# One tile per streamed weight block, and all leading products ahead of the remainders

## The chip, the cores and the metric

One core of a Trainium2 chip runs the whole program. The metric is the device time of one execution in microseconds (us).

## What is computed

One layer of a hybrid backbone block over 256 latent tokens and 256 context tokens of 2048 channels, everything in float32:

```python
u = rmsnorm(x, norm_g) * (1 + scale) + shift        # scale, shift, gt = silu(c) @ w_ada + b_ada
a, g, z_c, xr, z_r, gc, gr = split(u @ w_in)
v = a * sigmoid(g)                                  # 31-tap depthwise convolution along grid rows
v = silu(layernorm(conv(v)))                        # LayerNorm over the 2048 channels
y_conv = (v * silu(z_c)) @ w_conv_out
xc = conv4(xr); r, i = sigmoid(xc @ w_r), sigmoid(xc @ w_i)     # per direction, 16 blocks of 128
h = scan(a = exp(-8 r softplus(-lam)), b = sqrt(1 - a * a) * i * xc)
y_rnn = ((h_forward + h_backward) * silu(z_r)) @ w_rnn_out
y = sigmoid(gc) * y_conv + sigmoid(gr) * y_rnn
out = rmsnorm(x + gt * (y @ w_o), final_g)          # latents only
```

## The kernel before

The weights are streamed once, in 152 **blocks** of 128 x 2048 float32 (1 MB each): 136 that give 128 output channels (accumulator `acc`, products on line 234) and 16 for `w_o` (accumulators `o`, line 912). Every float32 product is made of three: an operand is split into a **leading part** (`whi`, a copy to a shorter format on ScalarE, ACT, line 180) and a **remainder** (`wlo` = weight - leading part, a subtraction on VectorE, DVE, line 185). TensorE (PE) adds `whi * xh + whi * xl + wlo * xh`, with `xh`, `xl` the two parts of the activations. A 128-channel block of 256 tokens has 16 channel tiles, so 32 products with `whi` and 16 with `wlo`.

Before, a block is two **half blocks** of 128 x 1024, each with its own load (SyncE's queue, SP, line 175), copy and subtraction, in pools of 4 buffers (`wraw`, `whl`). `slot()` runs one block: it issues the loads of block s + 3, then for each half 16 leading products and 8 remainders on PE, the copy of the same half of block s + 2 with the subtraction of the half before it (`stage_split`), the deferred steps (`run_deferred`) and some side work of ACT and DVE (`run_side`, with a budget in us). Each engine takes its instructions in the order of the program, so what stands ahead of a subtraction on DVE delays it.

Before the blocks comes the start: adaLN's sums from `w_ada` (64 loads of 512 KB into 8 buffers `adaraw`, products on line 209) alternate with the products of the first eight xr blocks, whose weights are 16 tiles of 512 KB (`wearly`). The blocks then go: xr and z_r with the recurrence (gates on line 472: float32 products of their own), the convolution's blocks a and g, `w_rnn_out` with its gate (blocks 104 to 119), `w_conv_out` (120 to 135), `w_o` (136 to 151).

Three pieces of side work matter below. **The LayerNorm** of the convolution ends inside block 108: its variance is summed over channels by PE (`tot`, line 717), copied to `var` (line 718), and `rsqrt` (ACT's Sqrt on line 196, then DVE's reciprocal and a Newton step on lines 197 to 201) gives `rstd`, with which DVE multiplies `cv` (line 767). **gt** of adaLN, 64 steps of 512 columns on DVE (line 820), reads tiles `gtraw` of 1024 columns, two of them loaded ahead, so four steps. **The evacuation of w_o** after each 512-column chunk is three DVE operations and one of ACT per token tile (lines 896 to 899).

Of the kernel before, what the change touches and what calls it, by code (L numbers as in the profile page):

```python
# [81 lines left out]
def block_kernel(ctx, tc, xcat, xtok, fgrow, par, wada, wgt, bgt, wearly, wall, wgate, out):  # L82
# [283 lines left out]
    def stage_load(s):  # L366
        if s < NS:
            raws[s] = [load(wall[s, h]) for h in range(2)]
# [655 lines left out]
```

## Time and profile before

| | |
|---|---|
| runs | 1146.59, 1145.22, 1146.40 us; median 1146.40 |
| profiled execution: span, first to last instruction | 1142.0 us |
| median of the runs less that span | 4.4 us |
| PE busy | 1121.5 us, 98% of the span |
| DVE busy | 924.9 us, 81% |
| ACT busy | 615.1 us, 54% |
| moved by DMA | 233.70 MB, 205 GB/s in the mean |

The profiled execution is recorded by its span alone; its own time is not listed apart from the runs, so the 4.4 us that lie around the span are those of the median run. How to read it: an engine's busy time says how much work it has; which engine sets the end is told by the chain of waits and by PE's list of waits. Starts are microseconds from the first instruction. L with a number is a line of the kernel before.

### The profile page before, as it was taken

The numbers are of one execution on the slowest core, as the hardware profiler recorded it, in microseconds if no ns is written. First come the engines' busy times: TensorE is split into PE (matmuls) and PEld (weight loads), VectorE is DVE, ScalarE is ACT, GpSimd is POOL, SyncE is SP. The second block draws the span as 40 slices with busy tenths as digits, with TensorE's granted clock in tenths as the row PEclk, the third lists the DMA queues.
The fourth block names the chain that finished last, engine by engine and source line by source line (L and its number), as shares of the span: only waits on it lengthen the run. The fifth ranks groups of instructions, "written<-read, shape, count | busy, mean of one in ns | idle before, by whom it ended". The sixth has DMA issues, their size and how long they took to land.

```text
span 1142.0 us, 20720 instructions
## 1 busy us (share of the span) xinstructions
PE 1121.5 (98%) x8316; PEld 1010.7 (88%) x8316; DVE 924.9 (81%) x1528; ACT 615.1 (54%) x838; POOL 0.2 (0%) x4
## 2 busy tenths in 40 slices
PE   6999999999999999999999999999999999999996
PEld 3777778777798989999999999999999999999885
DVE  5555588789879888899998989999985977888885
ACT  3222279777888877644454444443335854444443
POOL 0000000000000000000000000000000000000000
PEclk9999999999999999999999999999999999999999
DMA  9998444233346555465555555555554569888772
GB/s 376 400 409 324 189 134 134 102 125 125 106 141 196 160 167 164 143 209 184 185 185 171 183 183 185 175 183 178 181 188 150 169 205 324 316 310 285 268 279 93
DMA packets 67635, 233.70 MB, mean 205 GB/s; under 512 B 7505, under 2 KB 11729, under 8 KB 67153
## 3 DMA queue, kind: packets, MB, share of 16 engines
q1 hardware_dynamic: 67538, 232.37, 59.5%
q8 instruction: 65, 1.06, 0.4%
q14 instruction: 32, 0.26, 0.1%
HBM read 230.25 MB, written 2.10 MB: 203 GB/s over the span
## 4 chain that ended last, share of the span: by engine, by line
PE 98%; DVE 1%; DMA 0%; ACT 0%; issue 0%; ACTq 0%; SPq 0%; DVEq 0%
PE acc L234 72%; PE o L912 8%; PE xr L234 6%; PE gate L472 5%; PE ada L209 2%; PE part L234 2%; PE ms L228 1%; DMA hbuf<-in_xcat_dram 0%; PE tp L216 0%; PE mps L228 0%; PE gps L833 0%; PE vps L228 0%; DVE sq L259 0%; DVE wlo L171 0%; PE tot L279 0%
## 5 line engine op out<-in xcount | busy, mean ns | idle before, releaser
L234 PE MATMUL acc<-xh,whi 128*128 128x256 f32 (+1 forms) x2176 | 566.8, 296 | 0.0
L234 PE MATMUL acc<-xl,whi 128*128 128x256 f32 (+1 forms) x2176 | 552.3, 289 | 0.0
L180 ACT ACTIVATE whi<-raw 128x1024 fp32r<-128x1024 f32 x304 | 321.1, 1058 | 351.0 <-PE acc L234 277.3
L234 PEld LDWEIGHTS acc<-xh,whi 128*128 128x128 f32 x2176 | 416.7, 192 | 17.8 <-issue 9.3
L234 PEld LDWEIGHTS acc<-xl,whi 128*128 128x128 f32 x2176 | 416.9, 192 | 12.5 <-issue 7.7
L185 DVE TENSOR_TENSOR wlo<-raw,whi 128x1024 fp32r<-128x1024 f32 x304 | 371.0, 1223 | 70.0 <-ACT whi L180 66.3
L234 PE MATMUL acc<-xh,wlo 128*128 128x256 f32 (+1 forms) x2176 | 319.0, 289 | 0.0
L234 PEld LDWEIGHTS acc<-xh,wlo 128*128 128x128 f32 x2176 | 288.2, 192 | 5.0
L660 DVE SCALAR_TENSOR_TENSOR cv<-hbuf,pt,cv 128x196 f32<-128x196 f32 (+14 forms) x480 | 185.9, 451 | 13.0 <-ACT cv L651 12.6
L461 DVE SCALAR_TENSOR_TENSOR xc<-xr,pt,xc 128x510 f32<-128x510 f32 (+2 forms) x96 | 71.0, 742 | 0.2
L472 PE MATMUL gate<-xc,gw 128*128 128x512 f32 x128 | 60.0, 592 | 0.0
L820 DVE SCALAR_TENSOR_TENSOR zc<-gtraw,csil,zc 128x512 f32<-128x512 f32 x64 | 47.9, 748 | 5.4 <-DMA gtraw<-in_wgt_dram 4.7
L234 PE MATMUL xr<-xh,whi 128*128 128x512 f32 x96 | 40.4, 421 | 0.4 <-ACT xh L170 0.4
L912 PE MATMUL o<-whi,xh 128*128 128x512 f32 x128 | 40.6, 399 | 0.0
L498 DVE TENSOR_TENSOR_SCAN tr<-a,ti 128x512 f32<-128x512 f32 x32 | 39.1, 1223 | 0.7
L333 ACT ACTIVATE row<-ada 128x128 f32<-128x128 f32 (+1 forms) x22 | 7.2, 326 | 60.2 <-PE ada L209 60.2
L912 PE MATMUL o<-whi,xl 128*128 128x512 f32 x128 | 39.5, 389 | 0.0
L912 PE MATMUL o<-wlo,xh 128*128 128x512 f32 x128 | 39.4, 389 | 0.0
L234 PE MATMUL xr<-xl,whi 128*128 128x512 f32 x96 | 37.7, 392 | 0.2 <-DVE xl L171 0.2
L472 PEld LDWEIGHTS gate<-xc,gw 128*128 128x128 f32 x128 | 22.8, 189 | 17.0 <-issue 13.9
L234 PE MATMUL xr<-xh,wlo 128*128 128x512 f32 x96 | 37.4, 390 | 0.0
L209 PE MATMUL ada<-adaraw,csil 128*32 128x128 f32 (+1 forms) x704 | 32.5, 324 | 1.1 <-DVE sh L218 0.9
(169 smaller groups left out, 838.1 us busy)
## 6 DMA issues: line engine op xcount, KB each, us to landing
raw<-in_wall_dram SPq DMA_DIRECT2D x304, 512.0 KB, 3.5
adaraw<-in_wada_dram SPq DMA_DIRECT2D x64, 512.0 KB, 8.5
gtraw<-in_wgt_dram SPq DMA_DIRECT2D x32, 512.0 KB, 3.9
raw<-in_wearly_dram SPq DMA_DIRECT2D x16, 512.0 KB, 9.9
gw<-in_wgate_dram SPq DMA_DIRECT2D x32, 128.0 KB, 3.2
hbuf<-in_xcat_dram SPq DMA_DIRECT2D x2, 1024.0 KB, 7.1
cv<-in_xtok_dram SPq DMA_DIRECT2D x4, 512.0 KB, 5.8
out_dram<-cv SPq DMA_DIRECT2D x6, 256.0 KB, 2.6
```

What stands on the lines that cost most here:

```text
L180: A.activation(out=hi, in_=raw, func=AF.Copy)
L185: V.tensor_tensor(out=lo, in0=raw, in1=hi.bitcast(F32), op=SUB)
L209: PE.matmul(out=acc[g:g + 32, :w], lhsT=csil[:, k, :], rhs=raw[:, w * q:w * q + w], start=(k < 4), stop=(k >= KT - 4), tile_position=(0, g))
L228: PE.matmul(out=acc[32 * q:32 * q + 32, :], lhsT=ones[:, :32], rhs=x, start=(i < 4), stop=(i >= KT - 4), tile_position=(0, 32 * q))
L234: PE.matmul(out=acc, lhsT=w, rhs=x, start=(first and i == 0), stop=(last and i == n - 1))
L333: A.activation(out=row, in_=acc, func=AF.Copy)
L461: V.scalar_tensor_tensor(out=o, in0=i, scalar=w, in1=o, op0=MUL, op1=ADD)
L472: PE.matmul(out=acc, lhsT=u["gw"][:, c:c + 128], rhs=u["xc"], start=True, stop=True)
L498: V.tensor_tensor_scan(out=r(u["tr"]), data0=r(u["a"]), data1=r(u["ti"]), initial=0.0, op0=MUL, op1=ADD)
L660: V.scalar_tensor_tensor(out=o, in0=i, scalar=hdw[:, m * CW + j:m * CW + j + 1], in1=o, op0=MUL, op1=ADD)
L820: V.scalar_tensor_tensor(out=gt_chunk(c), in0=gt_raw[0][:, 512 * (k % 2):512 * (k % 2) + 512], scalar=csil[:, k, 0:1], in1=gt_chunk(c), op ...
L912: PE.matmul(out=acc, lhsT=y[:, k, 1, P * i:P * i + P], rhs=w[:, 512 * kk:512 * kk + 512], start=(k == 0 and w is hi and y is xh), stop=(k ...
```

## The change

A block is one tile of 128 x 2048, with one load of 1 MB, one copy and one subtraction (152 of each instead of 304), in 3 buffers of raw weights and 2 of each part (before: 4 halves of each). `staged()` replaces the two halves: the load of block s + 3; all 32 leading products; deferred steps and side work; the subtraction of block s + 1 and the copy of block s + 2; all 16 remainders; deferred steps and side work again. `w_o`'s blocks follow the same pattern, with both token tiles' leading products (8 each) ahead of both tiles' remainders (4 each). The early xr weights come in one load, one copy and one subtraction per group of one or two channel tiles.

The raw tiles take 8 KB more of each partition, and other buffers are cut: `adaraw` 8 to 6, the squares `sq` of the LayerNorm 8 to 4, `gtraw` from two tiles of 1024 columns to two of 512 (64 loads of 256 KB, two steps ahead), and `var` is dropped (ACT's Sqrt and DVE's Newton step read the sum `tot` in PSUM). PE's products are the same in number.

```diff
+RB = 3
...
-    wraw_p = ctx.enter_context(tc.tile_pool(name="wraw", bufs=4))
-    whl_p = ctx.enter_context(tc.tile_pool(name="whl", bufs=4))
+    wraw_p = ctx.enter_context(tc.tile_pool(name="wraw", bufs=RB))
+    whl_p = ctx.enter_context(tc.tile_pool(name="whl", bufs=2))
...
-    def load(src, n=1024):
-        raw = wraw_p.tile([P, 1024], F32, tag="raw", name="raw")
+    def load(src, n=2048):
+        raw = wraw_p.tile([P, 2048], F32, tag="raw", name="raw")
         SP.dma_start(out=raw[:, :n], in_=src)
         return raw
 
-    def wsplit_hi(raw):
-        hi = whl_p.tile([P, 1024], F32R, tag="whi", name="whi")
-        A.activation(out=hi, in_=raw, func=AF.Copy)
+    def wsplit_hi(raw, n=2048):
+        hi = whl_p.tile([P, 2048], F32R, tag="whi", name="whi")
+        A.activation(out=hi[:, :n], in_=raw[:, :n], func=AF.Copy)
         return hi
 
-    def wsplit_lo(raw, hi):
-        lo = whl_p.tile([P, 1024], F32R, tag="wlo", name="wlo")
-        V.tensor_tensor(out=lo, in0=raw, in1=hi.bitcast(F32), op=SUB)
+    def wsplit_lo(raw, hi, n=2048):
+        lo = whl_p.tile([P, 2048], F32R, tag="wlo", name="wlo")
+        V.tensor_tensor(out=lo[:, :n], in0=raw[:, :n], in1=hi[:, :n].bitcast(F32), op=SUB)
         return lo
 
-    def wsplit(raw, n=1024):
-        hi = whl_p.tile([P, 1024], F32R, tag="whi", name="whi")
-        lo = whl_p.tile([P, 1024], F32R, tag="wlo", name="wlo")
-        split(hi[:, :n], lo[:, :n], raw[:, :n])
-        return hi, lo
...
-        ada_p = st.enter_context(tc.tile_pool(name="ada", bufs=8))
+        ada_p = st.enter_context(tc.tile_pool(name="ada", bufs=6))
...
-                    wr = [load(wearly[k], P * NEARLY) for k in ks]
+                    wn = P * NEARLY * n
+                    wr = wraw_p.tile([P, 2048], F32, tag="raw", name="raw")
+                    SP.dma_start(out=wr[:, :wn].rearrange("p (k c) -> p k c", k=n), in_=wearly[:, k0:k0 + n, :])
...
-                    ws = [wsplit(w, P * NEARLY) for w in wr]
+                    hi = wsplit_hi(wr, wn)
+                    ws = (hi, wsplit_lo(wr, hi, wn))
...
-            raws[s] = [load(wall[s, h]) for h in range(2)]
-
-    late = []
-
-    def stage_split(s, h):
-        """the weights' leading parts; the remainders of the half block before"""
-        for k, raw, hi in late:
-            parts[k] = (hi, wsplit_lo(raw, hi))
-        late.clear()
+            raws[s] = load(wall[s])
+
+    def stage_hi(s):
         if s < NS:
-            raw = raws[s][h]
-            late.append(((s, h), raw, wsplit_hi(raw)))
-
-    def block_mms(s, acc, movh, movl, half):
-        hi, lo = parts.pop((s, half))
-        tr3 = []
-        for kk in range(8):
-            k = 8 * half + kk
-            w = hi[:, 128 * kk:128 * kk + 128]
-            tr3 += [(w, movh(k)), (w, movl(k))]
-        for kk in range(8):
-            tr3 += [(lo[:, 128 * kk:128 * kk + 128], movh(8 * half + kk))]
-        mm3(acc, half == 0, half == 1, tr3)
+            his[s] = wsplit_hi(raws[s])
+
+    def stage_lo(s):
+        if s < NS:
+            los[s] = wsplit_lo(raws.pop(s), his[s])
+
+    def block_mms(acc, ws, movs, first, last):
+        for k in range(KT):
+            for mov in movs:
+                PE.matmul(out=acc, lhsT=ws[:, P * k:P * k + P], rhs=mov(k), start=(first and k == 0 and mov is movs[0]),
+                          stop=(last and k == KT - 1))
+
+    def staged(s, leading, remainders, work):
+
+        stage_load(s + RB)
+        leading(his[s])
+        run_deferred()
+        work()
+        stage_lo(s + 1)
+        stage_hi(s + 2)
+        remainders(los[s])
+        del his[s], los[s]
+        run_deferred()
+        work()
...
-        """matrix products of block s, the weights of the blocks after it, side work"""
         acc = psum(f"acc{s}")
         view = acc[:, :N] if N == T else acc.rearrange("p (s t) -> p s t", s=2)
-        stage_load(s + 3)
-        for h in range(2):
-            block_mms(s, view, *mov, h)
-            stage_split(s + 2, h)
-            run_deferred()
-            run_side(budget / 2)
+        staged(s, lambda w: block_mms(view, w, mov, True, False), lambda w: block_mms(view, w, mov[:1], False, True),
+               lambda: run_side(budget / 2))
...
+    def chunk_mms(acc, w, seg, ys, kq, i, first, last):
+
+        for kk in range(4):
+            k = 4 * kq + kk
+            for y in ys:
+                PE.matmul(out=acc, lhsT=y[:, k, seg, P * i:P * i + P], rhs=w[:, 512 * kk:512 * kk + 512],
+                          start=(first and k == 0 and y is xh), stop=(last and k == KT - 1))
+
+    def chunk_slot(s, seg, accs, kq, work):
+
+        def leading(w):
+            for i in range(2):
+                chunk_mms(accs[i], w, seg, (xh, xl), kq, i, True, False)
+
+        def remainders(w):
+            for i in range(2):
+                chunk_mms(accs[i], w, seg, (xh,), kq, i, False, True)
+        staged(s, leading, remainders, work)
...
-            stage_split(1, 0)
+            stage_hi(1)
...
-    stage_split(1, 1)
...
-    def ln_total(dst):
+    def ln_total():
         tot = psum("tot")[:, :T]
         PE.matmul(out=tot, lhsT=sel4, rhs=ln["rstd"], start=True, stop=True)
-        V.tensor_copy(dst, tot)
+        return tot
 
     def ln_mean2():
-        ln_total(ln["mean"])
+        V.tensor_copy(ln["mean"], ln_total())
...
-        sq = tp2.tile([P, T], F32, tag="sq", name="sq", bufs=8)
+        sq = tp2.tile([P, T], F32, tag="sq", name="sq", bufs=4)
...
-        ln_total(ln["var"])
-        rsqrt(ln["rstd"], ln["mean"], ln["var"])
+        rsqrt(ln["rstd"], ln["mean"], ln_total())
...
-        raw = tp2.tile([P, 1024], F32, tag="gtraw", name="gtraw", bufs=GTB)
+        raw = tp2.tile([P, 512], F32, tag="gtraw", name="gtraw", bufs=GTB)
...
-        V.scalar_tensor_tensor(out=gt_chunk(c), in0=gt_raw[0][:, 512 * (k % 2):512 * (k % 2) + 512],
-                               scalar=csil[:, k, 0:1], in1=gt_chunk(c), op0=MUL, op1=ADD)
-        if n % 2:
-            gt_raw.popleft()
-            if n // 2 + GTB < 32:
-                gt_load(n // 2 + GTB)
+        V.scalar_tensor_tensor(out=gt_chunk(c), in0=gt_raw.popleft(), scalar=csil[:, k, 0:1],
+                               in1=gt_chunk(c), op0=MUL, op1=ADD)
+        if n + GTB < 4 * KT:
+            gt_load(n + GTB)
...
         for kq in range(2 if c == 3 else 4):
-            stage_load(s + 3)
-            for h in range(2):
-                for i in range(2):
-                    o_mms(accs[i], s, kq, h, i)
-                del parts[s, h]
-                stage_split(s + 2, h)
-                gt_steps(GTO)
+            chunk_slot(s, 1, accs, kq, lambda: gt_steps(GTO))
...
-    # the last two blocks: one token tile after the other
-    stage_split(NS, 0)
+
+    stage_lo(s + 1)
     for i in range(2):
         for q in range(2):
-            for h in range(2):
-                o_mms(accs[i], s + q, 2 + q, h, i)
+            chunk_mms(accs[i], his[s + q], 1, (xh, xl), 2 + q, i, False, False)
+            chunk_mms(accs[i], los[s + q], 1, (xh,), 2 + q, i, False, True)
```

**PE, where the LayerNorm's sum is made**, inside block 108 (`acc108`; `tot` is the sum, `whi`/`wlo` the weights' parts, numbers are tiles). Before:

```order
L234 MATMUL acc108_9733<-xl_97,whi_9612 128x256
L234 MATMUL acc108_9733<-xh_96,wlo_9653 128x256 x8
L717 MATMUL tot_9766<-rstd_5034,sel4_73 128x256
L234 MATMUL acc108_9733<-xh_96,whi_9655 128x256
L234 MATMUL acc108_9733<-xl_97,whi_9655 128x256
```

and with the change:

```order
L380 MATMUL acc108_9040<-xh_96,whi_8952 128x256
L380 MATMUL acc108_9040<-xl_97,whi_8952 128x256
L734 MATMUL tot_9075<-rstd_4738,sel4_73 128x256
L380 MATMUL acc108_9040<-xh_96,wlo_9018 128x256 x16
L380 MATMUL acc109_9115<-xh_96,whi_9020 128x256
```

The sum moves from the middle of the block's products to behind its last leading product; the remainders of block 109 then read `wlo_9090`.

**DVE in the same place** (`rstd_...<-vps` is the copy that feeds the sum, `wlo` are subtractions; `wlo_9727` and `wlo_9762` are the two halves of block 109). Before:

```order
L185 TENSOR_TENSOR wlo_9727<-raw_9582,whi_9699 128x1024
L739 COPY rstd_5034<-vps_9526 128x256
L185 TENSOR_TENSOR wlo_9762<-raw_9584,whi_9729 128x1024
L718 COPY var_5036<-tot_9766 128x256
L197 RECIPROCAL rstd_5034<-rstd_5034 128x256
L198 TENSOR_TENSOR mean_5035<-rstd_5034 128x256
L199 SCALAR_TENSOR_TENSOR mean_5035<-var_5036,mean_5035 128x256
L200 TENSOR_SCALAR mean_5035<-mean_5035 128x256
L201 TENSOR_TENSOR rstd_5034<-rstd_5034,mean_5035 128x256
L767 TENSOR_TENSOR cv_5031<-cv_5031,rstd_5034 128x256 x2
L771 TENSOR_TENSOR cv_5031<-cv_5031,zc_5032 128x256
L767 TENSOR_TENSOR cv_5031<-cv_5031,rstd_5034 128x256
```

and with the change:

```order
L186 TENSOR_TENSOR wlo_9018<-raw_8819,whi_8952 128x2048
L756 COPY rstd_4738<-vps_8853 128x256
L192 RECIPROCAL rstd_4738<-rstd_4738 128x256
L193 TENSOR_TENSOR mean_4739<-rstd_4738 128x256
L194 SCALAR_TENSOR_TENSOR mean_4739<-tot_9075,mean_4739 128x256
L195 TENSOR_SCALAR mean_4739<-mean_4739 128x256
L196 TENSOR_TENSOR rstd_4738<-rstd_4738,mean_4739 128x256
L783 TENSOR_TENSOR cv_4735<-cv_4735,rstd_4738 128x256 x2
L787 TENSOR_TENSOR cv_4735<-cv_4735,zc_4736 128x256
L783 TENSOR_TENSOR cv_4735<-cv_4735,rstd_4738 128x256
L186 TENSOR_TENSOR wlo_9090<-raw_8901,whi_9020 128x2048
```

Before, both halves of block 109's remainder are made ahead of the reciprocal, and the next subtraction behind it (`wlo_9806`) is of block 110. With the change the whole remainder of block 109 (`wlo_9090`) stands behind the reciprocal, the Newton step and four operations of the normalisation; the copy of `tot` is gone.

## Rows read from the trace of the kernel before

**Rows 1.** The page: busy time and instructions of the engines; the chain, share by engine.
```profile
PE 1121.5 (98%) x8316; PEld 1010.7 (88%) x8316; DVE 924.9 (81%) x1528; ACT 615.1 (54%) x838; POOL 0.2 (0%) x4
...
PE 98%; DVE 1%; DMA 0%; ACT 0%; issue 0%; ACTq 0%; SPq 0%; DVEq 0%
```

**Rows 2.** The last row of PE's list of waits (us in total, times, longest us).
```profile
PE xr L234 <- DVE xl L171: 0.2, 1, 0.2
```

**Rows 3.** Windows: us, then PE, PEld, DVE, ACT, POOL busy (instructions), clock, DMA share, GB/s.
```profile
0.00:100.00 100.00, 88.78 (x811) 60.35 (x812) 56.04 (x117) 30.59 (x51) 0.20 (x4) 1.00 0.98 386
...
600.00:800.00 200.00, 200.00 (x1660) 197.82 (x1659) 181.66 (x344) 87.47 (x105) 0.00 (x0) 1.00 0.56 180
```

**Rows 4.** PE in order of time, blocks 108 and 109 (start us, us, engine, line, operation).
```profile
880.28 0.28 PE L234 MATMUL acc<-xh,whi 128*128 128x256 f32 x1
...
883.15 0.59 PE L717 MATMUL tot<-rstd,sel 128*128 128x256 f32 x2
883.40 0.47 PE L234 MATMUL acc<-xh,whi 128*128 128x256 f32 x1
883.70 0.28 PE L234 MATMUL acc<-xl,whi 128*128 128x256 f32 x1
...
886.45 0.28 PE L234 MATMUL acc<-xh,whi 128*128 128x256 f32 x1
```

**Rows 5.** DVE in order of time, the same stretch.
```profile
883.78 0.42 DVE L718 COPY var<-tot 128x256 f32<-128x256 f32 x1 [1.95 <-PE tot L717]
885.36 1.75 DVE L197 RECIPROCAL rstd<-rstd 128x256 f32<-128x256 f32 x1 [1.15 <-ACT rstd L196]
...
890.63 1.22 DVE L185 TENSOR_TENSOR wlo<-raw,whi 128x1024 fp32r<-128x1024 f32 x1
```

**Rows 6.** ACT in order of time, the same stretch.
```profile
883.52 1.28 ACT L196 ACT_TABLE_LOAD   x1
884.82 0.51 ACT L196 ACTIVATE rstd<-var,epst 128x256 f32<-128x256 f32 x1
```

**Rows 7.** The page: the group of gt's steps (busy us, mean ns of one | idle before, releaser).
```profile
L820 DVE SCALAR_TENSOR_TENSOR zc<-gtraw,csil,zc 128x512 f32<-128x512 f32 x64 | 47.9, 748 | 5.4 <-DMA gtraw<-in_wgt_dram 4.7
```

**Rows 8.** PE in order of time at line 209, 49 to 66 us; the tile's landing times.
```profile
49.58 1.93 PE L209 MATMUL ada<-adaraw,csil 128*32 128x256 f32 x32
...
53.48 1.93 PE L209 MATMUL ada<-adaraw,csil 128*32 128x256 f32 x32
...
60.18 1.93 PE L209 MATMUL ada<-adaraw,csil 128*32 128x256 f32 x32
...
65.44 2.11 PE L209 MATMUL ada<-adaraw,csil 128*32 128x256 f32 x32
...
DMA to landing us min/median/max: 3.8/8.5/12.0
```

**Rows 9.** DVE, then PE, in order of time, behind the first column chunk of w_o.
```profile
1065.40 0.68 DVE L896 SCALAR_TENSOR_TENSOR hbuf<-o,zc 128x512 f32<-128x512 f32 x1
...
1071.02 1.22 DVE L185 TENSOR_TENSOR wlo<-raw,whi 128x1024 fp32r<-128x1024 f32 x1
...
1065.47 0.61 PE L912 MATMUL o<-whi,xh 128*128 128x512 f32 x2
...
1070.91 0.61 PE L912 MATMUL o<-whi,xh 128*128 128x512 f32 x2
```

**Rows 10.** PE in order of time behind a run of gates.
```profile
311.87 0.68 PE L234 MATMUL acc<-xh,whi 128*128 128x256 f32 x1
312.39 0.28 PE L234 MATMUL acc<-xl,whi 128*128 128x256 f32 x1
```

**Rows 11.** PE's first wait, and the windows of the start and of the end.
```profile
7.00 2.52 PE L228 MATMUL ms<-sq,ones 128*32 128x512 f32 x8 [7.00 <-DVE sq L259]
...
0.00:9.00 9.00, 2.00 (x8) 0.38 (x8) 3.00 (x12) 4.16 (x7) 0.20 (x4) 1.00 0.80 300
...
1134.00:1138.00 4.00, 0.00 (x0) 0.00 (x0) 2.70 (x10) 2.35 (x5) 0.00 (x0) 0.89 0.35 134
```

More of the change, by code (lines that the diff above doesn't have):

```diff
@@ L295, in products @@
             tr3 = []
-            for k, (hi, lo) in zip(ks, ws):
-                c = P * m
+            hi, lo = ws
+            for k in ks:
+                c = P * (m + NEARLY * (k - ks[0]))
                 tr3 += [(hi[:, c:c + P], xh[:, k]), (hi[:, c:c + P], xl[:, k]), (lo[:, c:c + P], xh[:, k])]
@@ L363, in block_kernel @@
     NS = len(seq)
[L364 removed]
+    raws, his, los = {}, {}, {}
     def stage_load(s):
         if s < NS:
[L368 to L390 removed]
+            raws[s] = load(wall[s])
+    def stage_hi(s):
+        if s < NS:
+            his[s] = wsplit_hi(raws[s])
[18 more added lines that the diff above has]
+        work()
     both = (lambda k: xh[:, k], lambda k: xl[:, k])
@@ L587, in block_kernel @@
     stage_load(1)
-    for h in range(2):
-        stage_split(0, h)
+    stage_hi(0)
+    stage_lo(0)
     pend = deque()
@@ L639, in open_ph2 @@
         p2 = cp.tile([P, KT, T], F32, name="p2")
-        for n in ("rstd", "mean", "var"):
+        for n in ("rstd", "mean"):
             ln[n] = tp2.tile([P, T], F32, tag=n, name=n, bufs=1)
@@ L905, in last @@
         return p2[:, 2 * i:2 * i + 2].rearrange("p a t -> p (a t)")
-    def o_mms(acc, s, kq, h, i):
-        hi, lo = parts[s, h]
-        for w, y in ((hi, xh), (hi, xl), (lo, xh)):
-            for kk in range(2):
-                k = 4 * kq + 2 * h + kk
-                PE.matmul(out=acc, lhsT=y[:, k, 1, P * i:P * i + P], rhs=w[:, 512 * kk:512 * kk + 512],
-                          start=(k == 0 and w is hi and y is xh), stop=(k == KT - 1 and w is lo))
     def finish(i):
@@ L941, in block_kernel @@
                 evac_o(c, i, accs[i])
-    stage_split(NS, 0)
+    stage_lo(s + 1)
     for i in range(2):
         for q in range(2):
-            for h in range(2):
-                o_mms(accs[i], s + q, 2 + q, h, i)
+            chunk_mms(accs[i], his[s + q], 1, (xh, xl), 2 + q, i, False, False)
+            chunk_mms(accs[i], los[s + q], 1, (xh,), 2 + q, i, False, True)
         evac_o(3, i, accs[i])
@@ L981, in _pack @@
                            .reshape(2 * n, P, 1024) for k, n in groups() for q in (1, 0)])
-    wgt = i["w_ada"][0][:, 4096:].reshape(8, 2, P, 4, 512).transpose(3, 0, 2, 1, 4).reshape(32, P, 1024)
+    wgt = i["w_ada"][0][:, 4096:].reshape(KT, P, 4, 512).transpose(2, 0, 1, 3).reshape(4 * KT, P, 512)
     def tiles(w):
@@ L987, in _pack @@
     mats = {"in": tiles(i["w_in"][0]), "conv": tiles(i["w_conv_out"][0]), "rnn": tiles(i["w_rnn_out"][0])}
-    wo = i["w_o"][0].reshape(4, 2, 2, P, 4, 512).transpose(4, 0, 1, 3, 2, 5).reshape(KT, 2, P, 1024)
-    wall = np.stack([wo[m] if a == "o" else mats[a][m].reshape(P, 2, 1024).transpose(1, 0, 2)
+    wo = i["w_o"][0].reshape(4, 4, P, 4, 512).transpose(3, 0, 2, 1, 4).reshape(KT, P, 2048)
+    wall = np.stack([wo[m] if a == "o" else mats[a][m].reshape(P, 2048)
                      for a, m in block_order()])
     e = mats["in"][BXR:BXR + NEARLY]
-    wearly = e.transpose(2, 1, 0, 3).reshape(KT, P, NEARLY * P)
+    wearly = e.transpose(1, 2, 0, 3).reshape(P, KT, NEARLY * P)
     g = np.stack([i["rnn_w_r"][0], i["rnn_w_i"][0]], axis=1)
```

1 line of the change is left out of this document (removed).

## The prediction

> **What bounds the kernel now.** I read the page first: PE is busy for 98% of the span, and 98% of the chain that ends last is PE's; DVE has 81%, ACT 54% [rows 1]. So an operation saved on DVE, ACT or SP is worth something only where PE waits for it. The list of PE's waits says where that is: its longest is the 7.0 us ahead of the very first product [rows 11], its last is 0.2 us [rows 2], all are in the first 26 us, and not one is a streamed weight, a copy `whi` or a subtraction `wlo`. In 600 to 800 us PE makes 1660 products in 200 us, 0.120 us each, with no gap between half blocks [rows 3]. A block of 48 products is then 5.76 us, its 32 leading products 3.84 us, its 16 remainders 1.92 us. The reader should see that the change touches nothing that PE waits for today. It can only lose time, where a part comes later than PE wants it, unless PE's own products get cheaper.
>
> **What gets cheaper, off the path.** 152 loads, copies and subtractions replace 304 of each. A DVE operation takes 0.42 us on 256 columns [rows 5] and a subtraction of 1024 columns 1.23 us, so about 1.05 us per 1024 columns and a fixed part of some 0.16 us; one of 2048 columns would take 2.29 us, an estimate between 2.2 and two of the old ones (2.46). That is some 0.16 us per block, 25 us of DVE in all, and for ACT likewise. I cost it at nothing: DVE runs ahead of PE, and PE hides it. Were DVE the cover that is gone, at most those 25 us would show; no row has PE waiting for DVE after the start.
>
> **What comes later: the subtraction.** Before, PE needs a half's remainder a third of a block after the half's leading part. Now block s + 1's whole remainder is made on DVE inside block s, behind the side work that stands there, and is wanted at the start of block s + 1 plus 3.84 us. In the mean block there is room: wlo's buffer is free at the start of block s, 9.6 us (5.76 + 3.84) before the remainder is wanted, and the subtraction takes 2.29. Three places have more than that in front of it.
>
> *The LayerNorm in block 108.* Block 108 starts at 880.28, block 109 at 886.45 [rows 4]. Before, DVE made both halves of block 109's remainder ahead of all that follows; the sum `tot` came at 883.15 [rows 4], DVE copied it at 883.78, Sqrt ran at 884.82 for 0.51 us [rows 6], the reciprocal at 885.36, and the next subtraction, of block 110, at 890.63 [rows 5]. With the change `tot` stands behind 32 leading products, at 880.28 + 3.84 = 884.12. The copy and its wait go: ACT can load its table (1.28 us [rows 6]) before the sum is there, and Sqrt starts 0.63 us behind `tot`, as the copy did (883.78 - 883.15), at 884.75, against 884.82. The reciprocal follows 0.54 us later, at 885.29. From there to the first subtraction DVE has the same operations as before, 890.63 - 885.36 = 5.27 us, so it begins at 890.56; but this is now block 109's, and it ends at 892.85. PE wants it at 886.45 + 3.84 = 890.29. **PE waits 2.6 us.** Bounds: 1.9 if the chain's two handovers, 0.63 and 0.54, are half as long and the subtraction takes 2.2; 3.4 if reading the sum from PSUM costs Sqrt and the Newton step the 0.42 us of the copy each. I take 2.6, since every duration in it stands in the rows. What is late next is block 110's subtraction: six operations of 0.42 us and 2.29 behind it, done at 897.7; PE, now 2.6 us later, wants it at 892.85 + 1.92 + 3.84 = 898.6. So one stall, not a series; PE never gets the time back.
>
> *The start.* DMA is 0.98 busy over the first 100 us [rows 3]. With 6 buffers a tile of `w_ada` can be asked for only when PE has read the tile six before it, not eight. A load lands 3.8 us after its issue at least [rows 8], and in this stretch they follow each other by 1.28 us (512 KB at some 410 GB/s; the mean of the window is 386 [rows 3]). PE's runs of four tiles start at 49.58, 53.48, 60.18 and 65.44, with 0.48 us per tile; the fourth took 2.11 instead of 1.93, so its last tile came just too late already [rows 8]. The last tile of the second run waits for the second tile of the first, read by 50.55: it lands at 54.4 to 55.1 and is wanted at 54.93. The last of the fourth waits for the second of the third, read by 61.15; eight tiles' worth of queue ahead of it puts it at 67.7, wanted at 66.9. I take 0.8 us in all; bounds 0 (the queue never runs empty) and 2.6 (two tiles' time, 2 x 1.28, which is what two buffers hold).
>
> *The evacuations of `w_o`.* Behind the first chunk DVE has 5.62 us of evacuation, 1065.40 to 1071.02, then (with the change) a step of gt, 0.75 [rows 7], and block 141's subtraction, done by 1074.06 at the latest. Block 140 starts at 1065.47 and block 141 at 1070.91 [rows 9]; two thirds of a block, 3.63 us, later the remainder is wanted, at 1074.54. Room 0.5 us, more if the first token tile's evacuation begins sooner. Three such places, no stall: 0, with 1 us each as the upper bound.
>
> The squares' 4 buffers, the single copy of early weights and block 1's copy (which must wait until PE has read the last early weights) are hidden: ACT is at 54% [rows 1], and PE's list shows no wait for ACT after the start. If that cover were gone, each would cost the copy's 2 us once.
>
> **The sum.** 2.6 + 0.8 = 3.4 us on a span of 1142.0, 1145.4. The median of the runs, 1146.4, lies 4.4 us over that span; I leave those alone: **1149.8 us**. The kernel's runs spread by 1.4 us, so about 0.2%, 2.3 us, is what a measurement can tell from no change: 1144.1 to 1148.7.
>
> **The rivals.**
>
> *No stall at the LayerNorm* (not slower). It decides at one point: the subtraction of block 109 must end by 890.29, 2.6 us sooner than I compute. Against it stands DVE's order; for it only that no row shows this chain with the sum read directly. Then the start alone is left: 1147.2. 0.13.
>
> *The gates' restart* (not slower, or faster). Behind a run of gates the first product takes 0.52 us until the next, 0.40 more than 0.12 [rows 10]; behind `tot`, half as wide, 0.18 more (883.40 to 883.70 [rows 4]). There are 31 such places, and with the change 17 of them are followed by remainders instead of leading products. If it is the next weights' load that is late there, remainders may pay less: at 0.18 instead of 0.40 the 17 give back 3.7 us, which with the stall is 1146.1; at nothing 6.8 us, 1143.0. Against it: the 0.18 goes with the narrower float32 product, so the cost seems to belong to the product before, not after. 0.13.
>
> *gt's steps take the subtraction's place* (slower still). Their tiles come now two steps ahead, not four, which is one block, 5.44 to 5.76 us; a weight load of 1 MB, 2.56 us, can stand between them in SP's queue. A tile needs 3.8 us alone, so up to 6.4: DVE would then lag up to 0.6 to 0.9 us per block. In the 16 blocks of `w_o` that is 12 us, of which the room of a block (9.6 - 2.29) takes 7; with `w_conv_out` too it is 24 less 7. That adds 5 to 17 us, and I put it at 8: 1158. For it: even before, gt's steps waited 4.7 us for their load [rows 7]. Against: in `w_conv_out` both loads stand ahead of the weights'. 0.09.
>
> *The clock.* PE waited 7.0 us before its first product, and the granted clock of the window 0 to 9 us is still 1.00; only behind the last product, in 1134 to 1138 us, does the mean fall, to 0.89 [rows 11]. So I expect a wait of 2.6 us to cost itself and no more. The Trainium skill, TensorE: Matmul & The Clock Gate, section "Why this matters for your kernels", warns against pauses between bursts of matmuls in the middle of a kernel, since the clock then drops to its lower level. The trace's first wait does not bear that out for this kernel. If it happened, the block behind the stall would run at 1.2 instead of 2.4 GHz, its 48 products at 0.24 us, 5.76 us more: 1155.6. 0.05.
>
> **How the numbers follow.** The forecast has 0.60, with a range of its own of 1148.3 to 1152.4 (1.9 to 3.4 and 0 to 2.6). Its lower edge and the two milder rivals reach below 1148.7: same 0.28; faster only by the restart, 0.05; slower 0.67. The range 1146.0 to 1155.0 leaves out gt's rival, the clock's and the best case of the restart, together some 0.18.
>
> **What would show it.** PE's list of waits must have one new entry of 2 to 3 us, on the subtraction, at 890 us, at a granted clock of 1.00; `tot` some 0.97 us later in its block; Sqrt starting at once behind it; entries on `adaraw` between 50 and 70 us of about 0.8 in all; none on `wlo` elsewhere, 0.120 us per product as before, and subtractions of 2.2 to 2.4 us. Waits on `wlo` in many blocks, DVE waiting for `gtraw`, or cheaper products behind the gates would make the prediction wrong, and so would a stall at 890 us of under 1.

## The result and the profile after

| | before | changed |
|---|---|---|
| median of the runs, us | 1146.18 (4 runs, 1145.22 to 1146.59) | 1158.48 (4 runs, 1156.39 to 1160.85) |
| ratio of the times | | 1.0106, 95% interval 1.0087 to 1.0125 |
| span of the profiled execution, us | 1142.0 | 1159.1 (its own time 1160.85) |
| PE busy, us | 1121.5 | 1131.1 |

The change makes the kernel 1.1% slower, 12.3 us between the medians and 17.1 us between the two profiled spans. The two differences are not the same because executions of one kernel differ by their mean granted clock: of the 55 runs of the kernel before beside the experiments, those at 0.998 took 1143.77 to 1144.65 us and those at 0.993 or 0.994 took 1146.12 to 1147.49, and the two profiled executions had 0.998 (before) and 0.990 (changed). The forecast was 1149.8, with a range up to 1155.0.

The page of the changed kernel: busy time, the chain by engine, and two groups (busy us, mean ns of one | idle before, releaser).

```profile
PE 1131.1 (98%) x8316; PEld 1016.2 (88%) x8316; DVE 909.4 (78%) x1370; ACT 591.5 (51%) x681; POOL 0.2 (0%) x4
...
PE 89%; DVE 5%; DMA 3%; ACT 1%; issue 1%; ACTq 0%; SPq 0%; DVEq 0%
...
L186 DVE TENSOR_TENSOR wlo<-raw,whi 128x2048 fp32r<-128x2048 f32 (+1 forms) x163 | 365.7, 2244 | 18.6 <-ACT whi L181 18.1
...
L836 DVE SCALAR_TENSOR_TENSOR zc<-gtraw,csil,zc 128x512 f32<-128x512 f32 x64 | 47.9, 749 | 23.1 <-DMA gtraw<-in_wgt_dram 19.7
```

Against [rows 1] the chain has lost 9% of PE to DVE, DMA and ACT, while PE's own busy time grew by 9.6 us with the same 8316 products: it was also slower. DVE is lighter by 15.5 us, as meant (a subtraction of 2048 columns takes 2.28 us; the mean in the row, 2.24, holds six of 1024 columns), and nothing is gained by it. gt's steps wait 19.7 us for their tiles, where it was 4.7 [rows 7].

PE's waits in the changed kernel that [rows 2] did not have:

```profile
PE o L589 <- DVE wlo L186: 4.2, 3, 3.0
PE acc L380 <- DVE wlo L186: 2.6, 2, 2.4
PE ada L204 <- DMA adaraw<-in_wada_dram: 1.8, 3, 0.6
```

How much later the first product of a block starts than in the kernel before tells where the time went:

| first product of block | before, us | changed, us | later by |
|---|---|---|---|
| 0 | 151.84 | 157.36 | 5.5 |
| 109 | 886.45 | 892.69 | 6.2 |
| 112 | 903.73 | 914.12 | 10.4 |
| 144 | 1088.13 | 1099.02 | 10.9 |
| 151 | 1124.39 | 1141.44 | 17.1 |

So there are three places: the start, the LayerNorm in block 108, and the evacuations of `w_o`.

**The LayerNorm.** PE in order of time:

```profile
890.35 0.59 PE L734 MATMUL tot<-rstd,sel 128*128 128x256 f32 x2
...
899.10 3.11 PE L380 MATMUL acc<-xh,wlo 128*128 128x256 f32 x16 [2.41 <-DVE wlo L186]
```

ACT:

```profile
887.21 1.28 ACT L191 ACT_TABLE_LOAD   x1
890.98 0.48 ACT L191 ACTIVATE rstd<-tot,epst 128x256 f32<-128x256 f32 x1 [2.49 <-PE tot L734]
```

DVE:

```profile
891.49 1.75 DVE L192 RECIPROCAL rstd<-rstd 128x256 f32<-128x256 f32 x1 [6.42 <-ACT rstd L191]
...
896.76 2.29 DVE L186 TENSOR_TENSOR wlo<-raw,whi 128x2048 fp32r<-128x2048 f32 x1
```

Sqrt starts 0.63 us behind the sum, the reciprocal 0.51 us later, the subtraction 5.27 us after that, and PE waits 2.41 us for it. What the forecast did not hold is in the windows behind it (us, busy times of the engines, granted clock, DMA share, GB/s):

```profile
898.00:900.00 2.00, 0.90 (x7) 0.90 (x8) 2.00 (x5) 1.53 (x2) 0.00 (x0) 0.99 0.00 0
900.00:902.00 2.00, 2.00 (x11) 2.00 (x10) 2.00 (x5) 2.00 (x5) 0.00 (x0) 0.50 0.88 274
902.00:904.00 2.00, 2.00 (x13) 2.00 (x13) 2.00 (x4) 1.59 (x1) 0.00 (x0) 0.66 0.60 250
904.00:906.00 2.00, 2.00 (x19) 2.00 (x18) 2.00 (x7) 1.88 (x4) 0.00 (x0) 1.00 0.78 201
```

The clock fell to its lower level (0.50) 0.9 us after PE resumed, and came back in 902 to 904 us: half of 2 us and a third of the next 2 are lost, 1.7 us of the 4.2 that block 112 loses against block 109.

**The start.** PE's runs of `w_ada` that had to wait for a tile:

```profile
58.89 0.64 PE L204 MATMUL ada<-adaraw,csil 128*32 128x256 f32 x8 [0.60 <-DMA adaraw<-in_wada_dram]
...
71.14 0.64 PE L204 MATMUL ada<-adaraw,csil 128*32 128x256 f32 x8 [0.52 <-DMA adaraw<-in_wada_dram]
...
72.42 0.64 PE L204 MATMUL ada<-adaraw,csil 128*32 128x256 f32 x8 [0.64 <-DMA adaraw<-in_wada_dram]
```

and the windows of the clock:

```profile
18.00:20.00 2.00, 1.25 (x34) 0.98 (x34) 1.38 (x8) 1.15 (x3) 0.00 (x0) 0.83 1.02 410
20.00:22.00 2.00, 2.00 (x10) 2.00 (x10) 0.33 (x2) 0.33 (x1) 0.00 (x0) 0.50 1.03 414
...
28.00:30.00 2.00, 2.00 (x8) 1.59 (x6) 0.68 (x3) 0.81 (x1) 0.00 (x0) 0.61 1.01 397
30.00:32.00 2.00, 2.00 (x37) 1.49 (x36) 1.38 (x2) 0.28 (x1) 0.00 (x0) 1.00 1.04 404
```

The clock was 0.50 for some 10 us from 19.3 us on. PE was 0.55 us later than before when it fell (0.28 of it at the first product) and 2.98 behind it, so the fall cost 2.4 us. The tiles cost another 2.5 us between 53 and 82 us, where the first run of products that [rows 8] shows at 53.48 starts 2.98 us later and the one at 76.32 (81.84 now) 5.52 later.

**The evacuations of `w_o`.** DVE behind the second chunk:

```profile
1099.09 0.75 DVE L836 SCALAR_TENSOR_TENSOR zc<-gtraw,csil,zc 128x512 f32<-128x512 f32 x1 [3.50 <-DMA gtraw<-in_wgt_dram]
1099.76 2.29 DVE L186 TENSOR_TENSOR wlo<-raw,whi 128x2048 fp32r<-128x2048 f32 x1
1101.96 0.74 DVE L836 SCALAR_TENSOR_TENSOR zc<-gtraw,csil,zc 128x512 f32<-128x512 f32 x1
1102.63 0.68 DVE L910 SCALAR_TENSOR_TENSOR hbuf<-o,zc 128x512 f32<-128x512 f32 x1
...
1108.24 0.75 DVE L836 SCALAR_TENSOR_TENSOR zc<-gtraw,csil,zc 128x512 f32<-128x512 f32 x1
1108.91 2.28 DVE L186 TENSOR_TENSOR wlo<-raw,whi 128x2048 fp32r<-128x2048 f32 x1
```

PE's next wait, and the windows behind it:

```profile
1111.24 3.50 PE L589 MATMUL o<-wlo,xh 128*128 128x512 f32 x8 [3.00 <-DVE wlo L186]
```

```profile
1112.00:1114.00 2.00, 2.00 (x6) 1.61 (x5) 2.00 (x2) 1.27 (x1) 0.00 (x0) 0.50 0.52 163
1114.00:1116.00 2.00, 2.00 (x8) 1.54 (x8) 1.50 (x2) 0.00 (x0) 0.00 (x0) 0.75 0.94 386
```

A step of gt waited 3.50 us for its tile. On DVE, behind that wait, stand a subtraction, another step, the whole evacuation (which could have begun some 3 us sooner), one more step, and only then the subtraction that PE wants. PE stood for 3.00 us, and the clock fell again, for another 1.7 us. The other two evacuations have the same pattern in small: a step waits 2.39 and 2.38 us for its tile just ahead of them, and PE stands 0.21 and 0.98 us behind them. gt's tiles land like this in the changed kernel:

```profile
DMA to landing us min/median/max: 2.5/3.9/6.2
```

The median, 3.9 us, is what it was before; but a step now has its tile asked for one block ahead, not two.

Added up, from the traces: waits on `wlo` 6.8 us, the start's waits on tiles 2.5, three stretches at the lower clock 2.4 + 1.7 + 1.7, the 0.55 us by which PE was late ahead of the first of them. That is some 15.7 of 17.1 us. The start's stretch is not shown to be the change's own: variants of the kernel before have it too (e2, e3, e10, e11). The rest is short restarts behind the stalls and two shifts of 0.3 and 0.4 us at blocks 19 and 42; what makes these was not looked into, but they are gone in e1 and e9, where the subtraction comes first.

### The profile page after: what moved, and what is told of

Same layout as the page of the kernel before. It is cut to its first block, busy times and chain, and to the rows that moved or that the text cites. A ratio compares the mean times of both kernels' runs of the same rounds, so it can differ in the third digit from the quotient of the medians.

```text
span 1159.1 us, 19850 instructions
## 1 busy us (share of the span) xinstructions
PE 1131.1 (98%) x8316; PEld 1016.2 (88%) x8316; DVE 909.4 (78%) x1370; ACT 591.5 (51%) x681; POOL 0.2 (0%) x4
## 3 DMA queue, kind: packets, MB, share of 16 engines
q8 instruction: 65, 1.06, 0.4%
## 4 chain that ended last, share of the span: by engine, by line
PE 89%; DVE 5%; DMA 3%; ACT 1%; issue 1%; ACTq 0%; SPq 0%; DVEq 0%
PE acc L380 69%; PE xr L229 6%; PE gate L476 5%; PE o L589 3%; DVE wlo L186 2%; PE ada L204 2%; PE part L229 2%; DMA gtraw<-in_wgt_dram 1%; DMA adaraw<-in_wada_dram 1%; PE ms L223 1%; DVE zc L836 1%; DMA hbuf<-in_xcat_dram 0%; PE tp L211 0%; PE mps L223 0%; ACT whi L181 0%
## 5 line engine op out<-in xcount | busy, mean ns | idle before, releaser
L380 PE MATMUL acc<-xh,whi 128*128 128x256 f32 (+1 forms) x2176 | 554.0, 293 | 0.0
L181 ACT ACTIVATE whi<-raw 128x2048 fp32r<-128x2048 f32 (+1 forms) x163 | 306.7, 1881 | 329.8 <-PE acc L380 263.6
L186 DVE TENSOR_TENSOR wlo<-raw,whi 128x2048 fp32r<-128x2048 f32 (+1 forms) x163 | 365.7, 2244 | 18.6 <-ACT whi L181 18.1
L380 PE MATMUL acc<-xh,wlo 128*128 128x256 f32 (+1 forms) x2176 | 305.8, 293 | 2.6 <-DVE wlo L186 2.6
L380 PEld LDWEIGHTS acc<-xh,wlo 128*128 128x128 f32 x2176 | 280.3, 192 | 19.6 <-issue 9.0
L677 DVE SCALAR_TENSOR_TENSOR cv<-hbuf,pt,cv 128x196 f32<-128x196 f32 (+14 forms) x480 | 182.3, 445 | 19.7 <-ACT cv L668 19.1
L836 DVE SCALAR_TENSOR_TENSOR zc<-gtraw,csil,zc 128x512 f32<-128x512 f32 x64 | 47.9, 749 | 23.1 <-DMA gtraw<-in_wgt_dram 19.7
L589 PE MATMUL o<-whi,xh 128*128 128x512 f32 x128 | 51.3, 401 | 0.0
L589 PE MATMUL o<-whi,xl 128*128 128x512 f32 x128 | 49.9, 389 | 0.0
L477 ACT ACTIVATE tr<-gate,hbr 128x512 f32<-128x512 f32 x32 | 21.9, 684 | 51.1 <-PE gate L476 51.0
L589 PE MATMUL o<-wlo,xh 128*128 128x512 f32 x128 | 33.7, 405 | 4.2 <-DVE wlo L186 4.2
```

What stands on the lines that cost most here:

```text
L181: A.activation(out=hi[:, :n], in_=raw[:, :n], func=AF.Copy)
L186: V.tensor_tensor(out=lo[:, :n], in0=raw[:, :n], in1=hi[:, :n].bitcast(F32), op=SUB)
L380: PE.matmul(out=acc, lhsT=ws[:, P * k:P * k + P], rhs=mov(k), start=(first and k == 0 and mov is movs[0]), stop=(last and k == KT - 1))
L477: A.activation(out=dst, in_=acc, func=AF.Tanh, scale=0.5, bias=hb[:, i:i + 1])
L589: PE.matmul(out=acc, lhsT=y[:, k, seg, P * i:P * i + P], rhs=w[:, 512 * kk:512 * kk + 512], start=(first and k == 0 and y is xh), stop=(la ...
L677: V.scalar_tensor_tensor(out=o, in0=i, scalar=hdw[:, m * CW + j:m * CW + j + 1], in1=o, op0=MUL, op1=ADD)
```

## The experiments

The kernel before was run beside each group: median 1144.65 (19 runs) beside e1 to e4, 1146.47 (17 runs) beside e5 to e8, 1145.30 (19 runs) beside e9 to e11. "Later" is the first product of a block against the profiled kernel before.

**e1: the subtraction first.** The changed kernel with

```diff
         leading(his[s])
+        stage_lo(s + 1)
         run_deferred()
         work()
-        stage_lo(s + 1)
         stage_hi(s + 2)
```

> The changed kernel with one line moved: the subtraction of block s + 1 stands straight behind the 32 leading products, ahead of the deferred steps and the side work. Theory 'order' (the stalls at the LayerNorm and behind the evacuations come from what stands ahead of the subtraction on DVE, and each stall of over 2 us also lowers the clock for some us): the waits of PE on wlo, 6.8 us in the changed kernel's trace, fall to under 1 us, block 110 is no longer 4.2 us further behind than block 109, block 146 no longer 4.6 us, the clock is 1.00 from 100 us to the last product, and the time falls by some 9 us to 1147 to 1151. Rival 'late tiles' (the subtraction is late because gt's tiles are, which stand two steps ahead only): the stall at 900 us goes, but that at 1111 us stays at 2 us or more, and the time falls by some 4 to 5 us only, to 1152 to 1154.

Measured: 1150.49 us (1148.78 to 1152.25), ratio 1.0049, 1.0037 to 1.0062: 8.0 us under the changed kernel's median, 6.5 by the two ratios. PE's waits:

```profile
PE o L589 <- DVE wlo L186: 1.6, 1, 1.6
...
PE acc L380 <- ACT whi L181: 0.7, 1, 0.7
```

Block 112 is 6.4 us late against 5.4 for block 109, instead of 10.4 against 6.2, and the clock is 1.00 in 890 to 915 us. So the LayerNorm's stall was the order on DVE. The other half speaks for the rival in part: 1.6 us of waiting on `wlo` remain behind an evacuation. The 0.7 us on ACT are new: block 110's copy now waits behind the LayerNorm's work there.

**e2: 6 buffers in the kernel before** (`name="ada", bufs=8` to `bufs=6`, nothing else).

> The kernel before with 6 buffers for w_ada instead of 8, nothing else. Theory 'buffers' (what block 0 starts later by is DMA waits of the start that the 6 buffers make): PE's waits on adaraw grow by 1.5 to 2.5 us, block 0 starts 2 to 3 us later at an unchanged clock, and the time rises by as much, to 1148 to 1149. Rival 'weights' (the 1 MB loads of the early weights and the deeper split, not the 6 buffers, delay the tiles): block 0 starts within 0.5 us of where it did. On the clock at the start (0.50 from about 19 to 29 us in the changed kernel's profile): if it comes from the start's own rhythm of PE work it may show here too in some runs, as two groups of times some 3 to 4 us apart.

Measured: 1148.74 us (8 runs, 1146.20 to 1149.84), ratio 1.0028, 1.0016 to 1.0040. PE's one new wait, to be held against 1.8 in the changed kernel:

```profile
PE ada L209 <- DMA adaraw<-in_wada_dram: 1.8, 4, 0.7
```

The same 1.8 us as in the changed kernel: the buffers do it, the early weights do not (e6 shows the other side: large early weights, 8 buffers, block 0 at its place). In this profile block 0 is 5.4 us later, because the clock fell at the start here too (0.50 in 26 to 30 us), in a kernel that has none of the rest of the change. Lowest against lowest it is 2.3 us (1146.20 against 1143.88); the one run with a granted clock of 0.998 took 1147.11, against 1143.88 to 1144.65 for the kernel before at 0.998.

**e3: gt's two steps in the kernel before.** Tiles of 512 columns, two of them, 64 loads:

```diff
-        raw = tp2.tile([P, 1024], F32, tag="gtraw", name="gtraw", bufs=GTB)
+        raw = tp2.tile([P, 512], F32, tag="gtraw", name="gtraw", bufs=GTB)
...
+        if n + GTB < 4 * KT:
+            gt_load(n + GTB)
```

> The kernel before with gt's tiles of 512 columns in two buffers (two steps ahead, 64 loads of 256 KB) as in the changed kernel, nothing else. Theory 'order': DVE waits for gtraw as in the changed kernel (10 to 25 us in all against 4.7), but the halves' subtractions have room and PE does not wait: time within 1 us of before. Rival 'late tiles': PE waits on wlo behind the evacuations of w_o by 2 us or more in all and the time rises by 2 to 6 us.

Measured: 1150.21 us (12 runs, 1145.27 to 1151.36), ratio 1.0040, 1.0028 to 1.0052. The wait of PE, then that of DVE:

```profile
PE o L910 <- DVE wlo L185: 3.3, 1, 3.3
```

```profile
DVE zc L820 <- DMA gtraw<-in_wgt_dram: 14.0, 15, 1.9
```

The rival holds, against my theory: halves of blocks have not room enough either. One stall of 3.3 us behind the third evacuation, and block 151 3.9 us later than block 144. The runs spread over 6 us, and four at the same granted clock of 0.997 over 4.1 us (1145.27 to 1149.39), so a stall of this size does not seem to come in every run. That it hangs on when a tile lands would fit, but is not shown.

**e8: the same loads of 256 KB, four steps ahead** (e3 with `GTB` 4).

> The kernel before with gt's tiles of 512 columns, 64 loads of 256 KB, but four of them ahead: the depth of the kernel before with the changed kernel's size of load. Theory 'depth' (steps ahead are what counts): DVE waits for gtraw no more than 6 us, no wait of PE on wlo, time within 1 us of before. Rival 'size' (twice as many, smaller loads behind SP's others are what is late): PE waits on wlo behind an evacuation as with two buffers, 3 us.

Measured: 1144.65 us (11 runs, 1143.86 to 1147.53), ratio 0.9997, 0.9987 to 1.0007, no wait of PE on `wlo` and none of DVE on `gtraw`. So it is the depth, and not the size or the number of the loads.

**e4: gt's third buffer in the changed kernel** (`GTB` 2 to 3, and 3 squares instead of 4 to make room).

> The changed kernel with a third buffer for gt's tiles (three steps ahead; one buffer of the LayerNorm's squares given for it, 3 instead of 4). Theory 'late tiles': DVE's waits for gtraw fall from 19.7 us to under 6 and the stall behind the second evacuation (3.0 us at 1111 us, with the clock at 0.5 behind it) falls under 1.5 us without a fall of the clock, 3 to 5 us less in time. Theory 'order' alone: the stalls behind the evacuations stay at about 4 us in all, since the evacuation itself stands ahead of the subtraction; the stall at 900 us stays in both at 2.4 us with the clock's fall.

Measured: 1154.56 us (1152.96 to 1156.35), ratio 1.0084, 1.0071 to 1.0096. PE's waits:

```profile
PE acc L380 <- DVE wlo L186: 2.6, 2, 2.4
...
PE vps L223 <- ACT sq L744: 1.0, 2, 0.5
```

No wait on `wlo` behind an evacuation is left: block 151 is as late as block 112, 10.9 us. So with three raw tiles it was gt's late tiles that made those stalls, and the order was their lever; e6 shows that another late tile can do the same. The LayerNorm's stall is there to the hundredth, 2.41 us, but this time the clock behind it stayed at 1.00, and blocks 109 to 112 lost 2.7 us instead of 4.2:

```profile
900.00:902.00 2.00, 0.92 (x7) 0.92 (x8) 2.00 (x5) 1.53 (x2) 0.00 (x0) 1.00 0.00 0
902.00:904.00 2.00, 2.00 (x19) 2.00 (x18) 2.00 (x5) 2.00 (x5) 0.00 (x0) 1.00 0.78 262
```

The third buffer's price is the squares': two waits of 0.5 us on `sq` with their restarts, 2.2 us at blocks 106 and 107.

**e7: the changed kernel once more.**

> The changed kernel once more, beside the others. Theory 'the start's clock is of the run, not of the kernel': the times lie in two or more groups some 3 to 5 us apart, as before (1156.4 and 1160.7), and a profile with the clock at 1.00 from 18 to 32 us has block 0 only 2.3 to 2.8 us later than in the kernel before, one with a fall there 5 to 6 us later.

Measured: 1159.04 us (1155.23 to 1161.05), ratio 1.0113, 1.0095 to 1.0130; the 9 times of the two groups of runs lie between 1155.2 and 1161.1, spread out rather than in two heaps, at granted clocks from 0.996 (the fastest) to 0.988. The profile repeats the first in its sums: waits of 4.3, 2.6 and 1.9 us on `wlo` of `w_o`, `wlo` and the tiles, the clock fallen at the start and behind the LayerNorm. But the wait behind the second evacuation is 1.57 us here, with the clock at 1.00, and that behind the third is 2.02 us, and there the clock fell:

```profile
1136.00:1138.00 2.00, 2.00 (x6) 1.21 (x5) 1.27 (x2) 0.42 (x1) 0.00 (x0) 0.50 0.00 0
```

No profile of the unaltered changed kernel came with a full clock at the start, so that part of the expectation was not tried here; e9 has one.

**e9: both repairs, e1 and e4.**

> Both repairs that the memory allows on the changed kernel: the subtraction straight behind the leading products and a third buffer for gt's tiles (for one of the squares' four). Theory 'three causes' (w_ada's 6 buffers, the order on DVE, gt's two steps): what is left is the start's 2.5 us of waits on adaraw, 0.9 us at block 110, and 1 to 2 us at blocks 106 and 107 that the squares' third buffer cost in the fourth experiment; no PE wait on wlo: 4 to 5 us slower than before in the same state of the clock, 1149 to 1151. Rival: the two repairs overlap or a fourth cause is left: PE waits on wlo of over 1 us remain, or the time is 1152 or more.

Measured: 1152.03 us (1149.94 to 1153.53), ratio 1.0064, 1.0050 to 1.0078. PE's waits:

```profile
PE ada L204 <- DMA adaraw<-in_wada_dram: 1.9, 3, 0.6
...
PE vps L223 <- ACT sq L744: 1.0, 2, 0.5
...
PE acc L380 <- ACT whi L181: 0.7, 1, 0.7
```

No wait on `wlo` at all, and the clock is 1.00 from where its record begins, at 10.7 us, to the last product. Block 0 is 2.7 us late (the tiles alone, with no fall of the clock), block 109 5.0 (the squares), block 112 6.0 and block 151 6.1: what is left of the causes, each in its place. The median is above what was expected, the profiled run, 1149.94, within it. That run had a granted clock of 0.998, the four others 0.996 to 0.993, so they ran longer at the lower clock; where, is not recorded. It is no faster than e1; the repair of gt was paid for with the squares.

**e5 and e6: the buffers back, with 2 raw tiles.** `RB` 2, `ada` 8, `sq` 8, `GTB` 4, and the load of block s + 3 behind the subtraction of block s + 1; e5 has the subtraction first, e6 where the change has it.

> One tile per block and all leading products first, as in the changed kernel, but with what it gave away put back: 8 buffers for w_ada, 8 for the squares, 4 for gt's tiles, paid for with 2 raw buffers instead of 3 (the load of block s + 3 is issued behind the subtraction of block s + 1, whose buffer it takes), and the subtraction straight behind the leading products. Theory 'order and buffers' (nothing in the large tiles themselves costs or gains time on PE): no PE wait on wlo, adaraw or gtraw beyond those of the kernel before, block 0 within 0.5 us of before where the clock is the same, about 0.9 us lost at block 110 as in the first experiment, time within 2 us of before. Rival 'large tiles' (1 MB loads and 2 us copies make something late whatever the buffers): 3 us or more slower, with PE waits on whi or wlo. Rival 'lighter engines' (152 fewer operations per engine pay off once nothing is late): faster by 2 us or more.

> The same as the kernel with all buffers put back, but the subtraction where the change has it, behind the deferred steps and the side work: the order alone. Theory: one stall of PE on wlo at the LayerNorm, 2.4 us, in some runs with 1 to 2 us more from a lower clock behind it, and stalls behind w_o's evacuations of at most 1 us each since gt's tiles are there: 2 to 4 us slower than the kernel with the subtraction first. Rival: stalls behind the evacuations stay over 2 us, so the order alone makes them.

Measured: e5 1152.56 us (1150.62 to 1154.61), ratio 1.0064, 1.0050 to 1.0078; e6 1155.31 us (1154.92 to 1156.66), ratio 1.0089, 1.0075 to 1.0103. e5's waits, then e6's:

```profile
PE acc L380 <- DVE wlo L186: 2.3, 1, 2.3
```

```profile
PE acc L380 <- DVE wlo L186: 4.5, 5, 2.4
PE o L589 <- DVE wlo L186: 3.2, 3, 1.6
```

The start is cured: block 0 is at its place within 0.1 us in e6, with 0.2 us of waits on tiles. But the two raw tiles make late places of their own, which the full set of buffers does not have: 2.5 us at block 118 in e5, 3.3 us up to block 44 in e6 (0.7 of it the shifts at blocks 19 and 42), and the stalls behind `w_o`'s evacuations are back in e6: 1.59 and 1.41 us on `wlo`, 5.4 us in all from block 145 to the end, more than the 1 us each that was expected. No step of gt waits for its tile here. Ahead of the first of these stalls it is a weight tile that is late, and the evacuation waits for its square behind the copy of that tile on ACT:

```profile
1096.03 1.92 ACT L181 ACTIVATE whi<-raw 128x2048 fp32r<-128x2048 f32 x1 [4.57 <-DMA raw<-in_wall_dram]
...
1098.59 0.69 DVE L913 TENSOR_TENSOR cv<-cv,zc 128x512 f32<-128x512 f32 x1 [2.81 <-ACT hbuf L912]
```

As a measure of the order alone the pair is inconclusive, except for the LayerNorm, where e6 loses 2.66 us and e5 0.99 between blocks 109 and 112. Large tiles with every buffer kept were not tried.

**e10 and e11: work for PE at the start of the kernel before.** Products that nothing reads, at three places between 15 and 20 us, two at each in e10, six in e11:

```diff
+        def fill():
+            for _ in range(2):
+                PE.matmul(out=fl, lhsT=pall("ident"), rhs=pall("ident"), start=True, stop=True)
```

> The kernel before with six more products of 128 x 128 that nothing reads, two each in three of PE's waits between 15 and 20 us (ahead of s, ahead of tot, behind tot). Theory 'PE's thin work at the start lets the clock fall' (in some runs the clock is 0.50 from about 19 to 29 us, which makes block 0 some 3 us later): the runs' times are all in the lower of the two groups of the kernel before (about 1144 against 1146.6), the median 1 to 2.5 us under it. Rival 'chance' (the fall does not depend on so little work): both groups stay, median within 0.7 us.

> The same with six instead of two products at each of the three places, some 5 us of PE work in waits of about 2 us: block 0 starts 2 to 3 us later by the products themselves. Theory 'thin work': the clock is 1.00 from 18 to 32 us in the profile and the times lie in one group, no more than 1 us wide, at about 1146 to 1147. Rival 'chance': two groups some 2.6 us apart.

Measured: e10 1146.07 us (11 runs, 1144.16 to 1147.53), ratio 1.0004, 0.9995 to 1.0013; e11 1148.83 us (9 runs, 1146.25 to 1149.37), ratio 1.0025, 1.0016 to 1.0035. e11's windows:

```profile
16.00:18.00 2.00, 2.00 (x23) 1.99 (x25) 0.35 (x1) 0.02 (x1) 0.00 (x0) 1.00 1.03 412
...
24.00:26.00 2.00, 0.74 (x18) 0.48 (x14) 1.96 (x4) 0.28 (x1) 0.00 (x0) 1.00 1.03 412
26.00:28.00 2.00, 1.42 (x34) 0.84 (x26) 1.23 (x3) 1.43 (x3) 0.00 (x0) 0.93 1.02 408
28.00:30.00 2.00, 2.00 (x6) 1.71 (x7) 0.51 (x3) 0.32 (x1) 0.00 (x0) 0.50 1.03 412
30.00:32.00 2.00, 2.00 (x27) 1.27 (x29) 1.55 (x2) 0.00 (x0) 0.00 (x0) 0.50 1.02 408
```

What I expected did not come: with PE busy through 16 to 22 us the clock was still 0.50 at 28 to 32 us, and both kernels' times keep their width of some 3 us. It does not refute the theory of thin work, though: the products filled the waits up to 20 us only, and PE was busy for just 0.74 and 1.42 us of the two windows ahead of this fall. The kernel before has a thin window there too (0.88 us in 22 to 24), and no fall in its profile. What decides at the start stays open.

## Why the prediction was wrong

**The base.** "The median of the runs, 1146.4, lies 4.4 us over that span; I leave those alone." Wrong: a run lies 1.75 us over its own span (1160.85 against 1159.1, 1149.94 against 1148.2), so the profiled kernel before took about 1143.8. Its runs go from there to some 1147 (beside e5: 6 of 17 under 1145, all at a granted clock of 0.996 or more; 10 over 1146, all at 0.994 or less). The median that I added to already held runs with more of the lower clock. This did not make the miss: as a median it was right (1146.18 with the fourth run), and from 1143.8 the same 3.4 us give 1147.2, further off. What failed are the terms that were added.

**The LayerNorm: right, and short by the clock.** 2.6 us were forecast, 2.41 measured; every link of that sum came as worked out (0.63, 0.51 where 0.54 was taken, 5.27 us), and e1 shows the cause. But "I expect a wait of 2.6 us to cost itself and no more" failed: in both profiles of the changed kernel it cost 1.7 us more. The rival that I gave 0.05 happened, at a third of its price (1.7 against 5.76). It does not happen each time: behind waits of 2.0 to 3.3 us the clock fell in four places of the profiles (the LayerNorm in both of the changed kernel, 2.41 us; an evacuation in each, 3.00 and 2.02) and stayed at 1.00 in four (3.27 in e3, 2.41 in e4, 2.27 at block 118 of e5, 2.41 at block 109 of e6). So the rule of the Trainium skill (TensorE: Matmul & The Clock Gate, "Why this matters for your kernels"), which speaks against pauses in the middle of a kernel, was the better guide than the one early wait of [rows 11], which lies ahead of the first product. The runs agree with it in four cases of those eight; the longest of the waits is not among the four.

And that early wait was misread. The trace's record of the clock begins only at 10.76 us, and a window without a record is shown as 1.00. The same products, up to 10.3 us and from 12 us on, say what the clock was (behind the bar: busy us, mean ns of one):

```profile
L228 PE MATMUL ms<-sq,ones 128*32 128x512 f32 x10 | 3.6, 1060 | 7.2 <-DVE sq L259 7.2
L228 PE MATMUL ms<-sq,ones 128*32 128x512 f32 x16 | 3.7, 604 | 0.4 <-ACT sq L261 0.4
```

Behind the wait of 7.0 us a product took 1.06 us, once the record shows 1.00 it took 0.60: PE began at the lower clock, and [rows 11] was no evidence that a wait leaves the clock alone.

**The start: right cause, a third of its size.** 0.8 us was forecast for the tiles, 2.5 measured, and 2.7 in e9 at a full clock, about the upper bound of 2.6; e2 shows the cause. I took the queue to be full behind every load; with 6 buffers DMA stood idle instead (0.92 busy in the first 100 us against 0.98 [rows 3]), and three late tiles, in two runs of products, added up.

**The evacuations: the step that failed most.** "Three such places, no stall: 0" held at none of the three: 4.2 us of waits (0.21, 3.00 and 0.98) and 1.7 of clock. I counted the evacuation and one step of gt, 0.75 us each, as if the tile were there, and put the tile's wait apart in a rival of 0.09 that was to make every block lag. It does not: between the evacuations the room of a block takes up a wait of 2.42 us (the one that ends at 1091.98) without a stall. It is enough that one wait of 3.5 us falls just ahead of an evacuation. e3 and e4 show it from both sides, and e8 that four steps ahead are enough in the kernel before.

**The rest held.** No gain from DVE's and ACT's lighter load, no cheaper restart behind the gates, no stall in the mean block, none from the early weights, 0.120 us per product, 2.28 us per subtraction (2.29 was estimated).

## What to carry to other kernels

A larger tile is paid for in depth somewhere: list what each cut buffer was ahead of, and price the wait by the load's landing time against the time of the steps ahead, at the place where most work stands behind it on that engine. Put the operation that the bottleneck waits for ahead of side work in program order, and not behind it: one moved line gave back some 7 us here. And take the base of a forecast from the time of the profiled execution itself, with the state of its clock, before a median is added to. A window that shows 1.00 is evidence of a full clock only where the trace has a record of it; the length of the products is the check.

## What was not expected of the hardware

At the start, PE's granted clock falls to 0.50 in nine of the 13 profiles, for some 3 to 10 us, from 19 to 28 us on, behind windows in which PE is partly idle; in four (before, e6, e8, e9) it does not, with such windows too. It made PE 2.4 us later in the changed kernel's profile. Filling PE's waits up to 20 us did not keep it from falling at 27.7 us (e11). A wait of 2.41 us in the same place of the same chain was followed by the lower clock in two profiles and by the full clock in two others (e4, e6); a wait of 2.02 us elsewhere was followed by the lower clock (e7), one of 3.27 us by the full clock (e3). What decides is not shown by these runs.
